# Strassen's seven block products for the up-projections of the second block's feed-forwards

## The chip, the cores and the metric

The kernel runs on one core of a Trainium2 chip. TensorE (PE) multiplies, VectorE (DVE), ScalarE (ACT) and GpSimd (POOL) do the elementwise work, and SyncE (SP) issues most of the loads. The metric is the time of one execution on the device, in microseconds (us); the time before is the median of three runs.

## The reference, cut to what matters

Two blocks of two layers each follow one another on 512 tokens of 1024 features, all in float32. The change touches only the feed-forward of the second block, which runs once in each of its two layers:

```python
# D_MODEL = 1024, D_FF = 2816, CONV_WIDTH = 3
def conv_glu_ffn(x, w_up, conv_w, conv_b, w_down):
    S = x.shape[1]
    h = x @ w_up
    a, b = h[..., :D_FF], h[..., D_FF:]
    ap = jnp.pad(a, ((0, 0), (CONV_WIDTH - 1, 0), (0, 0)))
    conv = conv_b + ap[:, 0:S] * conv_w[0]
    for j in range(1, CONV_WIDTH):
        conv = conv + ap[:, j:j + S] * conv_w[j]
    return (jax.nn.silu(conv) * b) @ w_down

# in each layer, behind the mixer:
x = x + conv_glu_ffn(rms_norm_2(x, norm2_g), w_up, conv_w, conv_b, w_down)
```

## The kernel before, in words

**Products.** Activations lie feature-major: a tile holds 128 features by 512 tokens. Every float32 operand of a large product is split into two float32r parts, hi (a rounded copy, ScalarE) and lo (the exact rest, `x - hi`, VectorE), and a product is three matmuls, hi·hi, hi·lo and lo·hi. A matmul has a stationary 128 by 128 block of weights and a moving tile of up to 512 tokens. All matmuls are issued by the helper `mm`, line L164.

**Weights.** `wget` (L269) loads a tile of 2048 numbers a partition into one of two buffers named raw (SP's queue), and `wsplit` (L256) makes whi (L260, ScalarE) and wlo (L261, VectorE), two buffers each. Up-projection tiles are 8 k-tiles by 256 columns; tiles of the product back (`w_down`) are 4 k-tiles by 256 columns.

**The feed-forward, `ffn2` (L1702).** The mixer's last product goes by `by_segment` (L311) over two segments of 256 tokens, and `rms` (L324) behind each segment sums the squares of the new residual and makes r = 1 / rms. `gained` (L1264) makes the feed-forward's input from `x * gain`, without r; r is multiplied in behind the up-products (L1722 on VectorE for the convolution's half, L1728 on GpSimd for the gate's). For each of 11 pairs of feature tiles, `up` takes one weight tile of the convolution's half and one of the gate's half: 4 output tiles of 8 k-tiles by 3 matmuls of 512 tokens, 96 matmuls. The convolution is one ScalarE instruction and two of VectorE (L1725, L1726), then SiLU; the gate multiplies (L1731), and the result is split into "g" (L358). `chunks` (L1143) takes the pairs in groups of 2, 2, 2, 2, 2 and 1; the product back of a group (`down`, four weight tiles of 24 matmuls of 512 tokens, added to the residual on VectorE, L1747) comes in one piece behind the first pair of the next group. The last group's product back goes by segment again (L1738).

**Order.** The order of the instructions on each engine is fixed when the kernel is built, by a planner that follows dependences, free buffers and the order of the program with its own estimates of durations. Each engine then works its list off in order. Small tiles of 256 columns come from a rotation of three buffers (`small`, L321), which the sums of squares use too; tiles of 512 columns for scratch come from a rotation of five (`tmp`).

## Time and profile before

| | |
|---|---|
| median of 3 runs | 3603.54 us (3602.54 to 3608.32) |
| span of the profiled execution | 3595.4 us |
| what lies around that span, against the median | 8.1 us |
| PE, weight loads, DVE, ACT, POOL busy | 96%, 80%, 65%, 38%, 22% of the span |
| feed-forward of the second block, each layer | 377 us of the span |

The profile is one execution. Busy shares are averages over stages with different limits; a stage's own row tells what limits it. A matmul's recorded duration overlaps the next one's, so the pace of PE is read from the distance of starts.

### The profile page before, as it was taken

The numbers are of one execution on the slowest core, as the hardware profiler recorded it, in microseconds if no ns is written. First come the engines' busy times: TensorE is split into PE (matmuls) and PEld (weight loads), VectorE is DVE, ScalarE is ACT, GpSimd is POOL, SyncE is SP. The second block draws the span as 40 slices with busy tenths as digits, with TensorE's granted clock in tenths as the row PEclk, the third lists the DMA queues.
The fourth block names the chain that finished last, engine by engine and source line by source line (L and its number), as shares of the span: only waits on it lengthen the run. The fifth ranks groups of instructions, "written<-read, shape, count | busy, mean of one in ns | idle before, by whom it ended". The sixth has DMA issues, their size and how long they took to land.

```text
span 3595.4 us, 46792 instructions
## 1 busy us (share of the span) xinstructions
PE 3446.1 (96%) x18150; PEld 2868.4 (80%) x18150; DVE 2319.3 (65%) x3809; ACT 1380.5 (38%) x2141; POOL 803.9 (22%) x812
## 2 busy tenths in 40 slices
PE   7998999999999999999999999979999999999998
PEld 5787888888888887877887887866888876778887
DVE  5458865557786765565757556797654569865454
ACT  4234545242222234355543334425422343453223
POOL 2232322320000022312321001563100126521101
PEclk9999999999999999999999999989999999899999
DMA  6376543423233323763433233443132252512232
GB/s 222 115 235 182 160 129 107 137 70 107 87 125 122 125 81 118 230 163 103 134 130 122 88 117 99 132 146 101 65 106 94 82 166 86 179 60 88 88 106 70
DMA packets 358589, 438.52 MB, mean 122 GB/s; under 512 B 41342, under 2 KB 310288, under 8 KB 358368
## 3 DMA queue, kind: packets, MB, share of 16 engines
q1 hardware_dynamic: 327648, 345.48, 32.0%
q0 software_dynamic: 19200, 71.17, 5.7%
q10 hardware_dynamic: 11520, 18.89, 1.6%
q8 instruction: 143, 2.34, 0.3%
q14 instruction: 78, 0.64, 0.1%
HBM read 363.78 MB, written 71.70 MB: 121 GB/s over the span
## 4 chain that ended last, share of the span: by engine, by line
PE 67%; DVE 8%; issue 2%; ACT 1%; DMA 1%; POOL 0%; DVEq 0%; SPq 0%; ACTq 0%; POOLq 0%
PE d L164 40%; PE s L164 19%; PE n L164 4%; DVE sc L1393 1%; PE o L164 1%; DVE wlo L261 1%; DVE m L1392 1%; PE g L164 1%; PE d L177 1%; PE b L177 1%; DVE hl L368 0%; DVE tmp L1324 0%; ACT whi L260 0%; DVE att L1486 0%; DVE pt L1554 0%
## 5 line engine op out<-in xcount | busy, mean ns | idle before, releaser
L164 PE MATMUL d<-h,whi 128*128 128x512 f32 (+2 forms) x2896 | 894.3, 392 | 16.3 <-DVE h L1271 6.1
L260 ACT CAST whi<-raw 128x2048 fp32r<-128x2048 f32 (+2 forms) x271 | 422.2, 1558 | 696.2 <-PE d L164 400.1
L164 PEld LDWEIGHTS d<-h,whi 128*128 128x128 f32 (+1 forms) x2896 | 539.8, 190 | 146.7 <-DVE h L1271 9.4
L261 DVE TENSOR_TENSOR wlo<-raw,whi 128x2048 fp32r<-128x2048 f32 (+2 forms) x255 | 484.3, 1899 | 234.9 <-ACT whi L260 233.2
L164 PE MATMUL d<-h,wlo 128*128 128x512 f32 (+2 forms) x1448 | 560.6, 391 | 1.4 <-DVE wlo L261 1.4
L164 PE MATMUL s<-h,whi 128*128 128x256 f32 (+3 forms) x2176 | 528.7, 335 | 12.8 <-ACT whi L260 6.5
L164 PEld LDWEIGHTS s<-h,whi 128*128 128x128 f32 (+1 forms) x2176 | 370.0, 189 | 60.4 <-ACT whi L260 6.8
L164 PE MATMUL s<-h,wlo 128*128 128x256 f32 (+3 forms) x1088 | 361.6, 333 | 2.3 <-DVE wlo L261 2.3
L164 PE MATMUL d<-g,whi 128*128 128x512 f32 (+1 forms) x1200 | 338.5, 374 | 6.1 <-DVE x L1070 2.3
L164 PEld LDWEIGHTS d<-h,wlo 128*128 128x128 f32 (+1 forms) x1448 | 275.1, 190 | 63.3 <-DVE wlo L261 1.8
L164 PEld LDWEIGHTS d<-g,whi 128*128 128x128 f32 x1200 | 216.9, 188 | 52.8 <-issue 2.8
L164 PEld LDWEIGHTS s<-h,wlo 128*128 128x128 f32 (+1 forms) x1088 | 205.7, 189 | 24.6 <-DVE wlo L261 3.0
L164 PE MATMUL n<-h,whi 128*128 128x512 f32 (+1 forms) x768 | 218.5, 367 | 4.6 <-ACT tmp L975 3.1
L164 PE MATMUL d<-g,wlo 128*128 128x512 f32 (+1 forms) x600 | 213.9, 373 | 0.0
L1728 POOL TENSOR_TENSOR ya<-ya,r 128x512 f32<-128x512 f32 x44 | 75.2, 1710 | 577.5 <-ACT ya L1727 577.5
L619 ACT ACTIVATE e<-s,sm 128x768 f32<-128x768 f32 (+1 forms) x160 | 130.9, 819 | 116.3 <-DVE sm L617 88.0
L164 PE MATMUL s<-ku,ku 96*128 96x512 f32 (+3 forms) x720 | 154.2, 345 | 17.6 <-ACT e L619 14.4
L164 PE MATMUL s<-g,whi 128*128 128x256 f32 (+1 forms) x688 | 168.2, 335 | 0.0
L617 DVE TENSOR_REDUCE sm<-s 128x1 f32<-128x768 f32 (+1 forms) x160 | 134.1, 844 | 50.3 <-PE s L164 48.7
L164 PEld LDWEIGHTS n<-h,whi 128*128 128x128 f32 x768 | 135.9, 192 | 26.6 <-ACT tmp L975 4.7
L164 PEld LDWEIGHTS s<-ku,ku 96*128 96x128 f32 (+1 forms) x720 | 120.7, 190 | 42.3 <-ACT e L619 18.8
L164 PE MATMUL d<-whi,h 128*128 128x256 f32 x768 | 147.9, 288 | 0.0
(472 smaller groups left out, 6315.6 us busy)
## 6 DMA issues: line engine op xcount, KB each, us to landing
raw<-in__w_up SPq DMA_DIRECT2D x88, 1024.0 KB, 5.1
raw<-in__w_in SPq DMA_DIRECT2D x53, 1024.0 KB, 5.4
raw<-in__w_down SPq DMA_DIRECT2D x80, 512.0 KB, 3.4
araw<-in__w_ada SPq DMA_DIRECT2D x28, 1024.0 KB, 5.4
raw<-in__w_out SPq DMA_DIRECT2D x16, 1024.0 KB, 5.0
raw<-in__w_ada SPq DMA_DIRECT2D x15, 1024.0 KB, 9.5
U<-qd SPq DMA_DIRECT2D x32, 256.0 KB, 4.6
qd<-hl POOLq DMA_DIRECT2D x14, 512.0 KB, 4.5
```

The source lines that it names most:

```text
L164: self.last = self.nc.tensor.matmul(*a, **k)
L177: return self.nc.tensor.transpose(*a, **k)
L260: self.nc.scalar.copy(hi, raw[:, 0:n])
L261: (self.nc.gpsimd if self.wpool else self.nc.vector).tensor_tensor(lo, raw[:, 0:n], hi.bitcast(F32), op=OP.subtract)
L617: nc.vector.tensor_reduce(m[:, 0:1], s, axis=AX.X, op=OP.max, negate=True)
L619: nc.scalar.activation(e, s, AF.Exp, bias=m[:, 0:1], accum_out=m[:, 1:2])
L1392: nc.vector.max(m8[t], sc[t])
L1393: nc.vector.match_replace(sc[t], m8[t], sc[t], TAKEN)
L1728: nc.gpsimd.tensor_tensor(t_, t_, r, op=OP.mult)
```

## The change

The up-projection of a weight tile is written as a product of 2 by 2 blocks: k in two halves of four k-tiles, columns in two halves of 128, tokens in two halves of 256. Instead of the eight block products, seven are made (a11, a12, a22 and the sums s1 to s4 of weight blocks, against blocks of the input and its sums T), each 4 k-tiles by 3 matmuls of 256 tokens, 84 matmuls a weight tile. The sums of weight blocks are four GpSimd instructions a tile, and their splits are two casts and two subtractions more; the results are put together by five VectorE instructions and two ScalarE copies from PSUM.

The first `NPLAIN` = 2 pairs of each layer (four weight tiles) are made without it, by `plain`, with matmuls of 256 tokens, all features of the first token half ahead of the second; meanwhile the generator `sums` makes T. The input is made by `halved` in place of `gained`, and it has r in it, so that the multiplications by r behind the products go. The products back of a group stand one by one behind the weight tiles of the next group. The product with s4 of a tile, `last`, is held back (`owed`) until the product back behind that tile has been issued, and the convolution or the gate of the tile follows it. The last output tile takes the place of the weight sums, and the load of the final gains moves from the start of `ffn2` to its end. Comments and docstrings go as well, so lines shift.

```diff
...
+NPLAIN = 2
...
+    def halved(self, x, r, scale, bias, fp, gtag, gbufs):
+        nc = self.nc
+        H = S // 2
+        B = [[[None] * 4 for _ in range(2)] for _ in range(2)]
+        for k in range(KD):
+            j, kk = k // 4, k % 4
+            hs = [self.t(fp, [P, S if j else H], F32R, "hb" if j else "ha", 8) for _ in range(2)]
+            B[j][0][kk] = [h[:, 0:H] for h in hs]
+            if j:
+                B[1][1][kk] = [h[:, H:S] for h in hs]
+            else:
+                both = self.t(fp, [P, S], F32R, gtag, gbufs)
+                B[0][1][kk] = [both[:, 0:H], both[:, H:S]]
+        T = [[self.t(fp, [P, 4, H], F32R, "ht", 8) for _ in range(2)] for _ in range(4)]
+        for n in range(2):
+            c = slice(n * H, (n + 1) * H)
+            for k in range(KD):
+                hi, lo = B[k // 4][n][k % 4]
+                v = self.small(H)
+                if k % 2:
+                    nc.gpsimd.tensor_tensor(v, x[k][:, c], r[:, c], op=OP.mult)
+                    if bias is None:
+                        nc.scalar.activation(v, v, AF.Copy, scale=scale(k))
+                    else:
+                        nc.scalar.activation(v, v, AF.Identity, scale=scale(k), bias=bias(k))
+                    nc.scalar.copy(hi, v)
+                    nc.vector.tensor_tensor(lo, v, hi.bitcast(F32), op=OP.subtract)
+                else:
+                    nc.vector.scalar_tensor_tensor(v, x[k][:, c], scale(k), r[:, c], op0=OP.mult, op1=OP.mult)
+                    if bias is None:
+                        nc.scalar.copy(hi, v)
+                        nc.vector.tensor_tensor(lo, v, hi.bitcast(F32), op=OP.subtract)
+                    else:
+                        nc.scalar.activation(hi, v, AF.Identity, bias=bias(k))
+                        nc.vector.scalar_tensor_tensor(lo, v, bias(k), hi.bitcast(F32), op0=OP.add, op1=OP.subtract)
+        def sums():
+            for kk in range(4):
+                u = []
+                for k in (kk, kk + 4):
+                    u.append(self.tmp(S))
+                    nc.gpsimd.tensor_tensor(u[-1], x[k], r, op=OP.mult)
+                    if bias is None:
+                        nc.scalar.activation(u[-1], u[-1], AF.Copy, scale=scale(k))
+                    else:
+                        nc.scalar.activation(u[-1], u[-1], AF.Identity, scale=scale(k), bias=bias(k))
+                b11, b12, b21, b22 = u[0][:, 0:H], u[0][:, H:S], u[1][:, 0:H], u[1][:, H:S]
+                a, b = self.tmp(S), self.tmp(S)
+                t1, t3, t4, t2 = a[:, 0:H], a[:, H:S], b[:, 0:H], b[:, H:S]
+                nc.gpsimd.tensor_tensor(t1, b11, b12, op=OP.subtract)
+                nc.gpsimd.tensor_tensor(t3, b22, b12, op=OP.subtract)
+                nc.gpsimd.tensor_tensor(t2, b22, t1, op=OP.add)
+                nc.gpsimd.tensor_tensor(t4, t2, b21, op=OP.subtract)
+                hi, lo = T[kk]
+                nc.scalar.copy(hi[:, 0:2, :], a.rearrange("p (i n) -> p i n", i=2))
+                nc.vector.tensor_tensor(lo[:, 0:2, :], a.rearrange("p (i n) -> p i n", i=2), hi[:, 0:2, :].bitcast(F32), op=OP.subtract)
+                nc.scalar.copy(hi[:, 2, :], t4)
+                nc.vector.tensor_tensor(lo[:, 2, :], t4, hi[:, 2, :].bitcast(F32), op=OP.subtract)
+                nc.scalar.activation(hi[:, 3, :], t2, AF.Copy, scale=-1.0)
+                nc.vector.scalar_tensor_tensor(lo[:, 3, :], t2, -1.0, hi[:, 3, :].bitcast(F32), op0=OP.mult, op1=OP.subtract)
+                yield
+        return B, T, sums()
+    def strassen_setup(self, B, T, fp):
+        self.sB, self.sT = B, T
+        self.sraw = self.t(fp, [P, 4, 512], F32, "sraw", 1)
+        self.shi = self.t(fp, [P, 5, 512], F32R, "shi", 1)
+        self.slo = self.t(fp, [P, 5, 512], F32R, "slo", 1)
+        self.fp, self.owed, self.odd = fp, None, 0
+    def plain(self, ws, n=2):
+        H = S // 2
+        pss = [self.pd() for _ in ws]
+        for t in range(2):
+            for (w, j), ps in zip(ws, pss):
+                for k in range(KD):
+                    bh, bl = self.sB[k // 4][t][k % 4]
+                    wh, wl = [x[:, k, j * P:(j + 1) * P] for x in w]
+                    for i, (a, b) in enumerate(((wh, bh), (wh, bl), (wl, bh))):
+                        self.mm(ps[:, t * H:(t + 1) * H], a, b, start=(k == 0 and i == 0), stop=(k == KD - 1 and i == 2))
+        return pss
+    def strassen_weights(self, ap2d, c0):
+        nc = self.nc
+        raw, self.ahead = self.ahead or self.wload(self.raw(), ap2d, 0, KD, c0, 256), None
+        rv = raw.rearrange("p (k n) -> p k n", k=KD)
+        blk = lambda t, i, j: t[:, 4 * j:4 * j + 4, P * i:P * i + P]
+        hi, lo = [self.t(self.wp, [P, 2048], F32R, tag, 2).rearrange("p (k n) -> p k n", k=KD) for tag in ("whi", "wlo")]
+        for v in (lambda t: t[:, :, 0:P], lambda t: blk(t, 1, 1)):
+            nc.scalar.copy(v(hi), v(rv))
+            nc.vector.tensor_tensor(v(lo), v(rv), v(hi).bitcast(F32), op=OP.subtract)
+        o, self.odd = self.odd, 1 - self.odd
+        sv = lambda t, i: t[:, i, :].rearrange("p (k n) -> p k n", k=4)
+        s2, s4, s3, s1 = [sv(self.sraw, i) for i in (o, 1 - o, 2, 3)]
+        nc.gpsimd.tensor_tensor(s3, blk(rv, 0, 0), blk(rv, 1, 0), op=OP.add)
+        nc.gpsimd.tensor_tensor(s1, blk(rv, 1, 0), blk(rv, 1, 1), op=OP.add)
+        nc.gpsimd.tensor_tensor(s2, s1, blk(rv, 0, 0), op=OP.add)
+        nc.gpsimd.tensor_tensor(s4, s2, blk(rv, 0, 1), op=OP.add)
+        for c, d in ((slice(2, 4), slice(3, 5)), (slice(0, 2), slice(1 - o, 3 - o))):
+            nc.scalar.copy(self.shi[:, d, :], self.sraw[:, c, :])
+            nc.vector.tensor_tensor(self.slo[:, d, :], self.sraw[:, c, :], self.shi[:, d, :].bitcast(F32), op=OP.subtract)
+        s2, s4, s3, s1 = [[sv(t, i) for t in (self.shi, self.slo)] for i in (1, 2 - 2 * o, 3, 4)]
+        return {"a11": [blk(hi, 0, 0), blk(lo, 0, 0)], "a12": [blk(hi, 0, 1), blk(lo, 0, 1)], "a22": [blk(hi, 1, 1), blk(lo, 1, 1)],
+                "s3": s3, "s1": s1, "s2": s2, "s4": s4}
+    def block_product(self, ps, w, x, first=True):
+        for k in range(4):
+            (wh, wl), (xh, xl) = [t[:, k, :] for t in w], x(k)
+            for i, (a, b) in enumerate(((wh, xh), (wh, xl), (wl, xh))):
+                self.mm(ps, a, b, start=(first and k == 0 and i == 0), stop=(k == 3 and i == 2), skip_group_check=not first)
+    def settle(self):
+        if self.owed is not None:
+            go, self.owed = self.owed, None
+            go()
+    def strassen(self, w, use):
+        nc = self.nc
+        H = S // 2
+        B, T = self.sB, self.sT
+        b = lambda j, n: lambda k: B[j][n][k]
+        t = lambda i: lambda k: [p[:, i, :] for p in T[k]]
+        row = lambda: self.t(self.fp, [P, S], F32, "row", 3)
+        bank = lambda: self.pd()[:, 0:H]
+        r0, pa, pb = row(), bank(), bank()
+        self.block_product(pa, w["a11"], b(0, 0))
+        nc.scalar.copy(r0[:, 0:H], pa)
+        self.block_product(pb, w["a12"], b(1, 0))
+        nc.vector.tensor_tensor(r0[:, 0:H], pb, r0[:, 0:H], op=OP.add)
+        self.settle()
+        r1, u2, pc, pdd, pf = row(), self.t(self.fp, [P, H], F32, "uu", 2), bank(), bank(), bank()
+        self.block_product(pc, w["s3"], t(1))
+        self.block_product(pdd, w["s1"], t(0))
+        self.block_product(pa, w["s2"], t(3), first=False)
+        nc.scalar.copy(u2, pa)
+        nc.vector.tensor_tensor(r1[:, 0:H], pc, u2, op=OP.add)
+        nc.vector.scalar_tensor_tensor(r1[:, H:S], r1[:, 0:H], -1.0, pdd, op0=OP.mult, op1=OP.subtract)
+        self.block_product(pf, w["a22"], t(2))
+        nc.vector.scalar_tensor_tensor(r1[:, 0:H], r1[:, 0:H], -1.0, pf, op0=OP.mult, op1=OP.subtract)
+        def last():
+            self.block_product(pdd, w["s4"], b(1, 1), first=False)
+            nc.vector.tensor_tensor(r0[:, H:S], pdd, u2, op=OP.add)
+            use(0, r0)
+            use(1, r1)
+        self.owed = last
     def ffn2(self, l, x):
         nc, a, col = self.nc, self.a, self.cols
         with ExitStack() as es:
             fp = self.pool(es, "fp", self.other())
...
+            gain = col["norm2"]
+            B, T, sums = self.halved(x, self.r2, lambda k: gain[:, k:k + 1], None, fp, "g", 12)
+            self.strassen_setup(B, T, fp)
             (w0, w1, w2), cb = self.cw, col["conv_b"]
...
+            gt, ya = {}, {}
+            def conv(f, u):
+                t_ = ya[f] = self.t(fp, [P, S], F32, "ya", 2)
+                nc.scalar.activation(t_, u, AF.Identity, scale=w2[:, f:f + 1], bias=cb[:, f:f + 1])
+                nc.vector.scalar_tensor_tensor(t_[:, 1:S], u[:, 0:S - 1], w1[:, f:f + 1], t_[:, 1:S], op0=OP.mult, op1=OP.add)
+                nc.vector.scalar_tensor_tensor(t_[:, 2:S], u[:, 0:S - 2], w0[:, f:f + 1], t_[:, 2:S], op0=OP.mult, op1=OP.add)
+                nc.scalar.activation(t_, t_, AF.Silu)
+            def gate(f, u):
+                t_ = ya.pop(f)
+                nc.vector.tensor_tensor(t_, u, t_, op=OP.mult)
+                gt[f] = self.split(fp, t_, S, "g", 12)
+            def up(p0, c0, use):
+                if p0 < NPLAIN:
+                    w = self.wget(a["w_up_2"][l], 0, KD, c0, 256)
+                    for j, ps in enumerate(self.plain([(w, 0), (w, 1)])):
+                        use(2 * p0 + j, ps)
+                    next(sums, None)
+                else:
+                    w = self.strassen_weights(a["w_up_2"][l], c0)
+                    self.strassen(w, lambda j, row: use(2 * p0 + j, row))
+            def down(f0, nk, g):
+                w = self.wget(a["w_down_2"][l], f0 * P, nk, g * 256, 256)
+                for j in range(2):
+                    m = 2 * g + j
+                    ps = self.pd()
+                    self.dense(w, j * P, P, gt, f0, nk, S, ps)
+                    nc.vector.tensor_tensor(x[m], ps, x[m], op=OP.add)
+            todo, f0 = [], 0
+            for npair in (2, 2, 2, 2, 2, 1):
+                per = len(todo) // (2 * npair)
+                for p0 in range(f0 // 2, f0 // 2 + npair):
+                    for c0, use in ((p0 * 256, conv), (F + p0 * 256, gate)):
+                        up(p0, c0, use)
+                        for _ in range(per):
+                            todo.pop(0)()
+                            self.settle()
+                todo = [lambda f=f0, g=g: down(f, 4, g) for g in range(4)]
+                f0 += 2 * npair
+            self.settle()
+            f0, nk = f0 - 2, 2
+            w = self.wget(a["w_down_2"][l], f0 * P, nk, 0, D)
+            self.banks(**(MIX2 if l < DEPTH - 1 else LAST))
             if l == DEPTH - 1:
...
+                gb = self.t(fp, [P, S], F32, "row", 3)
                 nc.gpsimd.dma_start(gb, a["final_norm_g_2"].rearrange("(o n) -> o n", o=1)[:, 512:D].to_broadcast([P, 512]))
...
+            self.by_segment(w, range(KD), gt, f0, nk, S, lambda m, ps, si, c: nc.vector.tensor_tensor(
+                x[m][:, c], ps, x[m][:, c], op=OP.add), self.rms(x, self.r2) if l < DEPTH - 1 else self.last_rows(x, fp, gb))
...
-                o = self.t(pool, [P, D], F32, "out", 2)
+                o = self.sraw.rearrange("p a n -> p (a n)")[:, t * D:(t + 1) * D]
...
```

## Rows read from the trace of the kernel before

**Rows 1.** The page's first part: busy time, share, instructions.

```profile
PE 3446.1 (96%) x18150; PEld 2868.4 (80%) x18150; DVE 2319.3 (65%) x3809; ACT 1380.5 (38%) x2141; POOL 803.9 (22%) x812
```

**Rows 2.** Windows: stretch, length, busy PE PEld DVE ACT POOL, clock, DMA.

```profile
2536.00:2913.00 377.00, 374.26 (x1673) 302.98 (x1671) 201.09 (x240) 125.25 (x145) 47.05 (x37) 1.00 0.30 95
3206.00:3583.00 377.00, 376.09 (x1705) 305.90 (x1704) 196.67 (x237) 124.88 (x150) 43.51 (x29) 1.00 0.26 85
2585.38:2652.58 67.20, 67.20 (x290) 53.98 (x289) 33.45 (x37) 19.79 (x20) 6.75 (x5) 1.00 0.30 94
```

**Rows 3.** Timeline of POOL in the first feed-forward: start, duration, work.

```profile
2585.38 2.87 POOL L1728 TENSOR_TENSOR ya<-ya,r 128x512 f32<-128x512 f32 x1 [12.76 <-ACT ya L1727]
2592.80 1.29 POOL L1728 TENSOR_TENSOR ya<-ya,r 128x512 f32<-128x512 f32 x1 [4.54 <-ACT ya L1727]
...
2652.58 2.87 POOL L1728 TENSOR_TENSOR ya<-ya,r 128x512 f32<-128x512 f32 x1 [13.88 <-ACT ya L1727]
```

**Rows 4.** Timeline of PE where matmuls have 256 columns, two places.

```profile
1838.18 0.28 PE L164 MATMUL d<-mg,wlo 128*128 128x256 f32 x1
...
1842.14 0.28 PE L164 MATMUL d<-mg,wlo 128*128 128x256 f32 x1
...
2898.20 0.28 PE L164 MATMUL d<-g,wlo 128*128 128x256 f32 x1
...
2903.80 0.28 PE L164 MATMUL d<-g,wlo 128*128 128x256 f32 x1
```

**Rows 5.** Groups by line and shape in 2556 to 2912 us: busy, mean ns.

```profile
L1747 DVE TENSOR_TENSOR x<-d,x 128x512 f32<-128x512 f32 x40 | 27.6, 690 | 44.4 <-PE d L164 44.4
L261 DVE TENSOR_TENSOR wlo<-raw,whi 128x1024 fp32r<-128x1024 f32 x20 | 24.5, 1225 | 2.9 <-ACT whi L260 2.4
L1726 DVE SCALAR_TENSOR_TENSOR ya<-u,colsw,ya 128x510 f32<-128x510 f32 x21 | 15.7, 749 | 0.7
...
L1738 DVE TENSOR_TENSOR x<-d,x 128x256 f32<-128x256 f32 x15 | 6.3, 422 | 2.9 <-PE d L164 2.9
L338 POOL TENSOR_TENSOR small<-small,tmp 128x256 f32<-128x256 f32 x6 | 4.7, 782 | 32.4 <-ACT tmp L336 28.0 <-ACT small L336 4.3
```

**Rows 6.** Timeline of DVE at three places.

```profile
2489.88 0.69 DVE L1625 TENSOR_TENSOR x<-d,x 128x512 f32<-128x512 f32 x1 [0.27 <-PE d L164]
...
2584.81 2.29 DVE L261 TENSOR_TENSOR wlo<-raw,whi 128x2048 fp32r<-128x2048 f32 x1 [1.86 <-ACT whi L260]
...
3012.53 6.77 DVE L261 TENSOR_TENSOR wlo<-raw,whi 128x2048 fp32r<-128x2048 f32 x1
```

**Rows 7.** Timeline of POOL at two of these places.

```profile
2489.49 1.30 POOL L1532 TENSOR_TENSOR qm<-qm,gt 128x512 f32<-128x512 f32 x1 [4.43 <-DVE gt L1531]
...
3012.27 2.41 POOL L1479 TENSOR_TENSOR qx<-qm,gt 128x1024 f32<-128x1024 f32 x1
3014.63 1.30 POOL L1477 TENSOR_TENSOR gt<-kb,gt 128x512 f32<-128x512 f32 x1
3015.88 1.26 POOL L1546 TENSOR_TENSOR pt<-pt 128x504 f32<-128x504 f32 x1
```

**Rows 8.** Timeline of PE where a feed-forward begins: first block's, then second's.

```profile
1848.94 0.59 PE L164 MATMUL n<-small,ones 128*128 128x256 f32 x2
1851.38 0.73 PE L164 MATMUL d<-h,whi 128*128 128x256 f32 x4 [1.85 <-ACT h L594]
...
1855.71 0.39 PE L164 MATMUL d<-h,whi 128*128 128x256 f32 x2
...
2536.13 0.58 PE L164 MATMUL d<-h,whi 128*128 128x256 f32 x2
```

**Rows 9.** Timeline of DVE: r of the second token half completed.

```profile
2551.86 0.42 DVE L395 SCALAR_TENSOR_TENSOR r<-small,r 128x256 f32<-128x256 f32 x1
```

**Rows 10.** Windows, the columns of Rows 2: the first block's feed-forward begins.

```profile
1849.00:1856.00 7.00, 5.09 (x22) 4.06 (x22) 6.84 (x11) 6.09 (x12) 2.37 (x4) 0.76 0.69 217
```

38 lines of the change are left out of this document (removed).

## Prediction, made before the changed kernel ran

> **What bounds the kernel now.** The page comes first: PE is busy for 96% of the span [rows 1]. That alone does not say that PE sets the pace, so the windows come next. Both feed-forwards of the second block last 377 us each with PE busy for 374 and 376, at the full granted clock (1.00, the 2.4 GHz level), while DVE works about half the time [rows 2]. The third reading is a pace. The GpSimd instruction behind a SiLU recurs at 2585.38 and 2652.58 [rows 3], 67.20 us apart: one group of two pairs, by the code 4 x 48 up-matmuls and 96 of the product back. 67.20 / 288 = 0.2333 us for a matmul of 512 tokens, without a hole. So here a matmul left out is time saved, until another engine becomes slower than PE.
>
> **What the products save.** The price of a matmul of 256 tokens stands in two places [rows 4]. From 2898.20 to 2903.80 there are 16 triples, 48 matmuls: 5.60 / 48 = 0.1167 us, exactly half of 0.2333. From 1838.18 to 1842.14 there are 33: 3.96 / 33 = 0.1200. The first has the same kind of operands in the same phase, so I take 0.1175. A weight tile is now 48 x 0.2333 = 11.20 us and becomes 84 x 0.1175 = 9.87 (9.80 to 10.08). Each layer has 22 weight tiles, 4 of them plain, so 36 tiles in all gain 1.33 us: **-47.9 us** (-40.3 to -50.4). The 8 plain tiles become 96 x 0.1175 = 11.28: **+0.6** (0 to +2.6).
>
> **Steady state: DVE and GpSimd.** A Strassen tile and the product back behind it will take PE 9.87 + 24 x 0.2333 = 15.47 us (16.80 before). In that time DVE has, by [rows 5], the lo parts of 3584 weights (3 x 1.23 and, at 512, 0.69: 4.4), of the product back's weights 1.23, two additions to the residual 1.38, five half-width instructions from PSUM 5 x 0.42 = 2.1, and the convolution 4 x 0.75 or the gate 4 x 0.69, 2.9 on average: 12.0 us, where 33.45 / 4 = 8.4 stand now [rows 2]. GpSimd has four sums at 1.29 [rows 3]: 5.2 us. ACT, now at 19.79 / 4 = 4.9 [rows 2], gains 1.5 casts of 1024 and two copies and stays near 8.
>
> 12.0 and 5.2 each fit into 15.47, but they don't always run side by side. The subtraction at 2584.81 ends at 2587.10 [rows 6]; the GpSimd instruction that starts in it takes 2.87 instead of 1.29 and ends 1.15 behind it [rows 3]. The other way round, a subtraction at 3012.53 that takes 2.29 elsewhere takes 6.77 [rows 6], while three GpSimd instructions in a row end at 3017.14 [rows 7]; it ends 2.16 after them. An addition from PSUM at 2489.88 takes its 0.69 [rows 6] inside a GpSimd instruction of 1.30 [rows 7]. So a DVE instruction with two inputs in SBUF and a GpSimd instruction exclude each other; one with an input in PSUM is free. The Trainium skill states this (SBUF — State Buffer, section Who interferes with whom): two SBUF inputs on VectorE contend with a GpSimd read, and the loser waits for the whole instruction. The trace agrees in both directions.
>
> Of DVE's 12.0 us 3.5 are free of it. If nothing of GpSimd's work were covered, the pair would need 17.1 us a tile, 1.65 more than PE: 36 x 1.65 = +59. If all fits, 0. I stay near the fit: DVE's free 3.5 us and its 3.5 idle us together exceed 5.2, GpSimd works a tile ahead, and the next tile's lo parts have from the end of a22 (8.5 us into the tile) to its end. A wait of half an instruction on each of four is about 2.5 us, and 14.5 still fit. I take 0.2 us a tile for collisions: **+7** (0 to +59).
>
> A weight tile's raw buffer is now held until GpSimd's last sum. On SP the next up-load waits for it, and the load of the next `w_down` tile stands behind; that tile is needed 9.9 us later, so I cost this at nothing; if GpSimd falls behind, it is part of the same delay. The load of the final gains moves behind GpSimd's last sums; the last product back (96 matmuls, 11.2 us) covers it.
>
> **Where a feed-forward begins.** Before, the up-products did not need r: the first stands at 2536.13 without idle time before it [rows 8], and r is complete only at 2552.28 [rows 9]. Now they wait for it. The nearest row is the first block's feed-forward, whose input has r in it: behind the last sums at 1848.94 PE idles 1.85 us, and only from 1855.71 do products follow at full pace [rows 8]. In those 6.77 us stand 12 products and 6 matmuls of sums, worth 12 x 0.12 + 6 x 0.25 = 2.9: 3.8 lost, and the granted clock of the stretch is 0.76, a mix of the 1.2 and 2.4 GHz levels [rows 10]. The changed kernel squares all eight tiles, and its `v` share three buffers with those sums, so the third `v` waits for the end of the second half's norm. DVE alone needs 16 x 0.42 + 8 x 0.47 + 2.29 + 1.5 = 14.3 us for the input, against 11.3 of the first plain tile: at least 3. If the three buffers pace the first half, it is 4.4 + (4 x 2.2 + 4 x 1.3) / 3 = 9, where 4.4 is my estimate for addition, square, sum and norm behind the last product (seven instructions of 0.4 to 0.8 in a row), 2.2 and 1.3 for the chains of an odd tile (GpSimd 0.78, two of ACT, DVE 0.42) and an even one (three of about 0.43), all after [rows 5]. I take 6 a layer: **+12** (+6 to +20).
>
> **T, late or not.** T must be there at the first Strassen tile's third product, 6 + 4 x 11.28 + 2.8 = 54 us after the beginning. GpSimd has by then 8 x 0.78 + 4 x (2 x 1.29 + 4 x 0.78) + 2 x 1.29 = 31.6; DVE 40 (input 10.5, three whole weight tiles 6.9, the first Strassen weights 3.1, convolution and gate 11.5, splits of T 6.1, norm 2). Taking turns all the time they need 71.7, 18 late; overlapped, none. I take 4 a layer: **+8** (0 to +36). What waits behind it is PE's whole list, since the first product back stands behind that tile.
>
> **The end.** Behind the last s4 DVE has the gate (3.8 us with ACT's casts), the last weights' lo 2.29 and four additions 2.8, covered by one product back of 5.6: at most 3.3 late. 1.5 a layer: **+3** (0 to +7).
>
> **The sum.** -47.9 + 0.6 + 7 + 12 + 8 + 3 = -17.3. On the profiled span 3595.4 it gives 3578; 8.1 us lie between that span and the median of the runs, so 3603.5 - 17.3 = **3586**.
>
> **Rivals.**
> - *DVE and GpSimd set the pace* (slower). Place: the 36 Strassen tiles, and the making of T. For it: [rows 6, 7], three GpSimd instructions in a row that let DVE through only at the end. Against: two of the four sums depend on the one before, DVE has 3.5 us a tile that need no turn, and nothing that it makes is due at once. All in turns it is +59 in place of +7: 3638. It decides from 0.2 + 17.3 / 36 = 0.7 us of stall a tile on. By the skill's page cited above, applied to every pair of instructions, this would be the outcome.
> - *The beginnings cost double* (+24, and T +16): about 3606, no change. For it: three buffers for a chain that has four of its own in the first block. Against: whole PE tiles stand ready to hide the second half.
> - *All is hidden*: -50.4 + 6 = 3559 to 3568. Against it: PE's idle time in [rows 8].
> - *A matmul of 256 tokens isn't half price in this mix*, because each loads its own weights. 84 of them cost as much as before at 11.20 / 84 = 0.133 us; both rows are below. The Trainium skill (TensorE: Matmul & The Clock Gate, section LDWEIGHTS) prices a load of 128 columns by the columns alone, an estimate of 107 ns at any width of the moving tile; not overlapped, that would double a 256-token matmul and cost some 300 us. The trace does not agree: 0.1167 from start to start.
>
> **How the numbers follow.** PE-bound with the boundary costs above, 3568 to 3596: 0.55, my forecast. All hidden: 0.08. DVE and GpSimd in turns, wholly or in part, 3600 to 3640: 0.22, a quarter of it within 0.2%. Beginnings double: 0.12. Matmuls dearer: 0.03. About 0.2%, 7 us, is what a measurement of this kernel can tell from no change. Faster by more: 0.55 + 0.08 = 0.63. Same: 0.12 + 0.05 = 0.17. Slower: 0.17 + 0.03 = 0.20. The range for 8 in 10 leaves out the fastest part of the hidden case and the slower half of the turns: 3563 to 3620; the forecast's own is 3568 to 3596.
>
> **What the profile after would show.** A group of four Strassen tiles and four products back in 61.9 us instead of 67.20, with PE busy throughout; 84 matmuls a tile at 0.117 to 0.120. DVE near 12 us a tile plus some 2.5 of longer instructions beside GpSimd's 5.2. PE idle for some 6 us at both beginnings, ended by `hi` or `lo` of the input, and a few before the first product with T, ended by a split of T. I am wrong if groups take 65 us or more with PE waiting for lo parts or POOL sums, or if the idle time at a beginning passes 12 us.

## The result, and the profile after

The changed kernel takes 3639.6 us (median of 4 runs, 3637.9 to 3641.7), the kernel before beside it 3603.7: ratio 1.0099 [1.0085, 1.0112]. It is slower by 36 us, and outside the range of 3563 to 3620. The profiled span is 3636.2 us, 40.8 longer than before.

The page's first part, against [rows 1]:

```profile
PE 3435.1 (94%) x19782; PEld 2929.3 (81%) x19782; DVE 2501.4 (69%) x4093; ACT 1483.0 (41%) x2377; POOL 1038.3 (29%) x976
```

Windows of the two feed-forwards and of the first one's Strassen stage, columns as in [rows 2]:

```profile
2537.00:2930.00 393.00, 365.96 (x2479) 332.13 (x2478) 292.42 (x378) 175.97 (x266) 161.28 (x113) 0.98 0.28 90
3230.00:3624.00 394.00, 367.79 (x2513) 334.86 (x2512) 287.57 (x382) 178.73 (x275) 162.51 (x112) 0.98 0.26 83
...
2607.00:2911.00 304.00, 292.08 (x1945) 262.21 (x1945) 219.15 (x285) 123.98 (x175) 111.59 (x67) 1.00 0.30 94
```

PE has less to do and takes longer: 26 to 27 us of each stretch are idle where [rows 2] had 1 to 3. For a ledger I call *lost* the length of a stretch minus its matmuls at the pace of [rows 2], 0.2333 us for 512 columns and half of it for 256; so it holds idle time and also what matmuls take beyond that pace. The feed-forward runs from the mixer's last product to its own last one; two numbers are the two layers, in us.

| | before | after | change |
|---|---|---|---|
| length | 374.4, 376.2 | 393.3, 393.9 | +36.6 |
| matmuls at that pace | 370.9, 371.3 | 345.3, 345.9 | -51.0 |
| lost in the first 50 us | 1.1, 0.4 | 21.7, 19.3 | +39.5 |
| lost after that | 2.4, 4.5 | 26.4, 28.7 | +48.2 |

So the products saved what was forecast, and two other things cost more: the beginnings, and the steady state. Of what is lost after the first 50 us, 24.1 and 24.3 lie between the first Strassen product and the last, 2.2 and 4.3 behind the last, and nothing ahead of the first. (The other 4 us of the span lie outside the feed-forwards.)

**Steady state.** Waits from 2600 to 2880: what the DMA queue of SP, PE and PE's weight loads waited for (us in total, times, longest):

```profile
SPq L266 <- DVE wlo L1799: 213.6, 16, 14.4
...
PE d L165 <- ACT whi L1798: 6.0, 13, 0.8
PE d L165 <- DVE wlo L1799: 5.4, 13, 0.4
...
PEld d L165 <- ACT whi L1798: 11.7, 13, 1.2
PEld d L165 <- DVE wlo L1799: 8.3, 14, 0.6
```

The timelines of SP, POOL, ACT and DVE around one tile (start, duration, work):

```profile
2720.40 0.37 SPq L266 DMA_DIRECT2D raw<-in__w_up  x1
2723.02 0.37 SPq L266 DMA_DIRECT2D raw<-in__w_down  x1
2737.66 0.37 SPq L266 DMA_DIRECT2D raw<-in__w_up  x1
...
2725.70 1.84 POOL L1804 TENSOR_TENSOR sraw<-raw 128x512 f32<-128x512 f32 x1 [10.11 <-DMA raw<-in__w_up]
...
2730.70 2.15 POOL L1807 TENSOR_TENSOR sraw<-sraw,raw 128x512 f32<-128x512 f32 x1
...
2732.89 1.05 ACT L1809 CAST shi<-sraw 128x1024 fp32r<-128x1024 f32 x1 [2.03 <-POOL sraw L1807]
2733.85 0.36 ACT L1846 COPY uu<-d 128x256 f32<-128x256 f32 x1
2734.11 1.57 ACT L1798 CAST whi<-raw 128x1024 fp32r<-128x1024 f32 x2
...
2733.97 1.23 DVE L1810 TENSOR_TENSOR slo<-sraw,shi 128x1024 fp32r<-128x1024 f32 x1 [2.27 <-ACT shi L1809]
...
2735.45 1.22 DVE L1799 TENSOR_TENSOR wlo<-raw,whi 128x1024 fp32r<-128x1024 f32 x1
...
2736.92 0.69 DVE L1799 TENSOR_TENSOR wlo<-raw,whi 128x512 fp32r<-128x512 f32 x1
```

Read them as a circle. The tag `raw` has two buffers, and up-tiles and `w_down` tiles take them in turn, so every up-tile has the same one. Its load is issued at 2720.40, lands and lets GpSimd begin at 2725.70 (5.3 us); the four sums end at 2732.85 (7.15, by turns with VectorE, for 4 x 1.29 = 5.2 alone); only then come the cast and the subtractions that also read `raw`, because in the lists of ScalarE and VectorE they stand behind the casts of the sums; the last ends at 2737.61 (4.8), and at 2737.66 the next load goes out. That is 17.26 us, and PE's work for a tile and its product back is 15.4. From 2651.31 to 2822.81 there are eleven such loads, 17.15 us apart on average: PE does not set the pace, and waits a little for each `whi` and `wlo`. Of the 24.1 us lost in this stage 11.9 are idle PE (304.00 - 292.08); the granted clock is 1.00, and the rest stands inside the recorded times of matmuls, whose weight loads waited for the same two tiles.

**The beginning.** Timelines of PE, ACT, DVE and POOL; the mixer's last product is at 2537.05, against [rows 8, 9]:

```profile
2544.40 2.08 PE L165 MATMUL n<-small,ones 128*128 128x256 f32 x4 [6.88 <-DVE small L339]
2548.32 1.01 PE L165 MATMUL d<-ha,whi 128*128 128x256 f32 x3 [1.85 <-ACT ha L1736]
...
2537.26 1.88 ACT L261 CAST whi<-raw 128x2048 fp32r<-128x2048 f32 x1
2539.16 1.28 ACT L393 ACT_TABLE_LOAD   x1
2540.45 0.47 ACT L393 ACTIVATE r<-n,eps 128x256 f32<-128x256 f32 x1
...
2539.17 2.29 DVE L262 TENSOR_TENSOR wlo<-raw,whi 128x2048 fp32r<-128x2048 f32 x1 [1.19 <-ACT whi L261]
...
2544.27 0.94 DVE L396 SCALAR_TENSOR_TENSOR r<-small,r 128x256 f32<-128x256 f32 x1
...
2541.61 3.32 POOL L339 TENSOR_TENSOR small<-small,tmp 128x256 f32<-128x256 f32 x4 [7.37 <-ACT small L337]
```

Before, products followed without a hole. Now PE idles 6.88 us for the second half's squares and 1.85 for the first `ha`. Ahead of the norm stand the split of the second plain weight tile (1.88 and 2.29 us) and a table load of 1.28, and VectorE's instruction of 0.42 us [rows 9] takes 0.94 beside GpSimd's additions. PE is idle for 13.9 us of the first 50 (its window stands under "The beginnings": 36.13 busy); the other 7.8 of the 21.7 lost are matmuls slower than the pace of [rows 2], at a granted clock of 0.83. No product with T waits.

### The profile page after: what moved, and what is told of

Same layout as the page of the kernel before. It is cut to its first block, busy times and chain, and to the rows that moved or that the text cites. A ratio compares the mean times of both kernels' runs of the same rounds, so it can differ in the third digit from the quotient of the medians.

```text
span 3636.2 us, 51011 instructions
## 1 busy us (share of the span) xinstructions
PE 3435.1 (94%) x19782; PEld 2929.3 (81%) x19782; DVE 2501.4 (69%) x4093; ACT 1483.0 (41%) x2377; POOL 1038.3 (29%) x976
## 4 chain that ended last, share of the span: by engine, by line
PE 51%; DVE 13%; DMA 5%; issue 4%; POOL 4%; ACT 2%; SPq 0%; DVEq 0%; ACTq 0%; POOLq 0%
PE d L165 25%; PE s L165 18%; PE n L165 4%; DMA raw<-in__w_up 3%; POOL sraw L1807 2%; DVE wlo L262 1%; DVE wlo L1799 1%; POOL sraw L1805 1%; PE o L165 1%; DVE sc L1394 1%; POOL sraw L1806 1%; PE g L165 1%; DVE m L1393 1%; ACT shi L1809 1%; PE d L178 1%
## 5 line engine op out<-in xcount | busy, mean ns | idle before, releaser
L261 ACT CAST whi<-raw 128x2048 fp32r<-128x2048 f32 (+2 forms) x235 | 353.4, 1504 | 487.6 <-PE s L165 247.3
L262 DVE TENSOR_TENSOR wlo<-raw,whi 128x2048 fp32r<-128x2048 f32 (+2 forms) x219 | 405.4, 1851 | 182.8 <-ACT whi L261 182.0
L165 PE MATMUL d<-h,whi 128*128 128x512 f32 (+2 forms) x1456 | 451.8, 392 | 16.4 <-DVE h L1272 6.1
L165 PEld LDWEIGHTS s<-h,whi 128*128 128x128 f32 (+1 forms) x2176 | 370.9, 190 | 59.0 <-ACT whi L261 6.8
L165 PE MATMUL d<-g,whi 128*128 128x512 f32 (+1 forms) x1328 | 369.2, 365 | 6.1 <-DVE x L1071 2.3
L165 PEld LDWEIGHTS d<-h,whi 128*128 128x128 f32 (+1 forms) x1456 | 272.1, 192 | 84.7 <-DVE h L1272 8.9
L165 PE MATMUL d<-h,wlo 128*128 128x512 f32 (+2 forms) x728 | 283.1, 392 | 1.3 <-DVE wlo L262 1.3
L1810 DVE TENSOR_TENSOR slo<-sraw,shi 128x1024 fp32r<-128x1024 f32 x72 | 94.7, 1315 | 137.8 <-ACT shi L1809 137.8
L339 POOL TENSOR_TENSOR small<-small,tmp 128x256 f32<-128x256 f32 x36 | 28.3, 786 | 521.2 <-ACT tmp L337 496.1
L165 PEld LDWEIGHTS d<-h,wlo 128*128 128x128 f32 (+1 forms) x728 | 139.8, 192 | 31.6 <-DVE wlo L262 1.8
L165 PE MATMUL d<-ht,shi 128*128 128x256 f32 x864 | 158.7, 283 | 0.0
L1804 POOL TENSOR_TENSOR sraw<-raw 128x512 f32<-128x512 f32 x36 | 54.9, 1526 | 360.0 <-DMA raw<-in__w_up 292.1
```

The source lines that it names most:

```text
L165: self.last = self.nc.tensor.matmul(*a, **k)
L261: self.nc.scalar.copy(hi, raw[:, 0:n])
L262: (self.nc.gpsimd if self.wpool else self.nc.vector).tensor_tensor(lo, raw[:, 0:n], hi.bitcast(F32), op=OP.subtract)
L1804: nc.gpsimd.tensor_tensor(s3, blk(rv, 0, 0), blk(rv, 1, 0), op=OP.add)
L1810: nc.vector.tensor_tensor(self.slo[:, d, :], self.sraw[:, c, :], self.shi[:, d, :].bitcast(F32), op=OP.subtract)
```

## Experiments

All are edits of the changed kernel, and their ratios go to runs of the kernel before beside them. Lost is counted as above: in the first 50 us of the two feed-forwards, and in the whole of both.

| kernel | us | lost, first 50 | lost, all |
|---|---|---|---|
| before | 3603.7 | 1.1, 0.4 | 8.4 |
| after | 3639.6 | 21.7, 19.3 | 96.1 |
| e1_raw2 | 3598.3 | 23.2, 21.0 | 56.0 |
| e2_order | 3596.6 | 23.2, 19.4 | 54.9 |
| e3_dve | 3596.3 | 23.3, 21.0 | 56.4 |
| e4_vbuf | 3635.1 | 15.5, 13.7 | 91.7 |
| e5_both | 3590.7 | 15.5, 12.9 | 48.6 |
| e6_rready | 3594.1 | 16.4, 18.5 | 47.3 |
| e7_split | 3590.9 | 15.2, 15.8 | 44.1 |
| e8_noT | 3592.6 | 19.2, 17.9 | 49.5 |
| e9_keep | 3594.2 | 20.1, 18.9 | 51.1 |
| e10_lateR | 3606.2 | 19.1, 21.1 | 62.3 |
| e12_noT_late | 3583.0 | 14.1, 13.1 | 39.3 |
| e13_split_rready | 3582.4 | 14.5, 14.8 | 41.6 |
| e14_lateR_noT | 3580.3 | 10.9, 14.9 | 38.4 |
| e15_rready_noT | 3570.3 | 8.2, 8.0 | 28.3 |
| e16_lateR_tlate | 3608.1 | 14.7, 17.1 | 67.3 |
| e17_split_tlate | 3587.8 | 15.4, 16.5 | 46.1 |

The time is a median over runs, what is lost comes from the one profiled execution. For all of the changed kernels here the time is 3540 to 3547 us plus what is lost: the ledger accounts for it to a few us, and differences below that are not read.

### The circle around the raw buffer

**e1_raw2**: the `w_down` tiles come in two halves through scratch tiles, so that up-tiles have both raw buffers; every other instruction stays.

```diff
-w = self.wget(a["w_down_2"][l], f0 * P, nk, g * 256, 256)
+hi, lo = ...
+for i in range(2):
+    raw, c = self.wload(self.tmp(S), ...), slice(512 * i, 512 * i + 512)
+    nc.scalar.copy(hi[:, c], raw)
+    nc.vector.tensor_tensor(lo[:, c], raw, hi[:, c].bitcast(F32), op=OP.subtract)
```

> Weights of the products back are loaded in two halves into scratch tiles, so that up-projection tiles have both raw buffers; all sums, splits and products stay. Theory A (one raw buffer is loaded, summed by GpSimd, cast, and only then reloaded, a closed loop of about 17.1 us a tile): a Strassen tile with its product back falls from about 17.1 us to 15.4 to 15.7, and the whole to about 3595 to 3605. Theory B (VectorE and GpSimd exclude each other, 12.0 + 5.2 = 17.2 us of work a tile): all that work stays, so the tile stays near 17.1 and the whole near 3640.

**e2_order**: nothing but the order; the two casts to `shi` and the two subtractions to `slo` of a tile are issued behind those to its own `whi` and `wlo`.

```diff
+with self.tc.issue_after(ia.ins), self.tc.issue_after(iv.ins):
     nc.scalar.copy(self.shi[:, d, :], ...)
     nc.vector.tensor_tensor(self.slo[:, d, :], ...)
```

> The casts and subtractions of a tile's weight sums are issued behind those of the tile's own weights on ScalarE and VectorE; nothing else changes. Theory A: the raw buffer is free once GpSimd's sums are done instead of 4.8 us later, the loop is 5.3 + 7.2 = 12.5 us, and the tile falls to 15.4 to 15.7, the whole to about 3595 to 3605. Theory B: the same work takes the same turns, tile near 17.1, whole near 3640.

**e3_dve**: the four sums on VectorE (`nc.gpsimd` to `nc.vector` in four lines).

> The four weight sums of a tile are made by VectorE instead of GpSimd. Theory A: the loop loses GpSimd's 7.2 us and gains about 3 on VectorE, 5.3 + 3 + 4.8 = 13, so PE paces again unless VectorE, now at 14.8 us of work a tile, falls behind: tile 15.5 to 16.2, whole 3600 to 3620. Theory B: no turns are left, 14.8 us of VectorE fit into 15.4, the same 15.5. If neither holds and the order of the lists is what costs, it stays at 3640.

All three broke the circle: ratios to before 0.999 [0.9981, 0.9999], 0.9982 [0.9973, 0.9992] and 0.9985 [0.9975, 0.9995]; lost in the Strassen stage 2.6 to 2.8 us a layer where 24.2 stood. Windows of that stage, of e1_raw2, e2_order and e3_dve:

```profile
2609.00:2891.00 282.00, 282.00 (x1940) 261.10 (x1940) 234.71 (x302) 127.84 (x194) 117.19 (x64) 1.00 0.29 94
```

```profile
2613.00:2895.50 282.50, 282.50 (x1944) 261.58 (x1944) 230.57 (x285) 124.75 (x175) 98.56 (x65) 1.00 0.32 101
```

```profile
2615.00:2897.00 282.00, 282.00 (x1941) 261.13 (x1940) 233.75 (x348) 124.14 (x175) 0.00 (x0) 1.00 0.32 101
```

PE has no hole, though in the first two GpSimd and VectorE do all their work, with their turns. So the turns do not set the pace by themselves; in the changed kernel they lengthened the sums inside the circle. In e2_order eleven up-loads from 2652.75 to 2808.28 are 15.55 us apart. e3_dve fits both theories; e1_raw2 and e2_order decide between them, since both leave the turns in place.

### The beginnings

**e4_vbuf** gives `v` of `halved` buffers of its own (those of `row` and `uu`, idle then) in place of the three that the norm uses:

```diff
-v = self.small(H)
+v = self.t(fp, [P, S], F32, "row", 3)[:, 0:H] if k % 2 else self.t(fp, [P, H], F32, "uu", 2)
```

> The scratch tiles of the feed-forward's input come from five buffers of their own instead of the three that the sums of squares use. Theory S1 (those three hold the input back): the first product with the input comes about 2 us earlier, the next two stretches lose some 5 us less, and the whole falls by 10 to 15 us to about 3627. Theory S2 (the norm itself is late, behind a weight split, a table load and turns with GpSimd): less than 4 us in all, about 3637.

**e5_both** is e2_order and e4_vbuf together.

> The sums' casts behind the tile's own (as in e2_order) and v in buffers of its own (as in e4_vbuf), together. If the closed loop of the raw buffer only hid what v's buffers give back at the two beginnings, both gains add: e2_order stood at 3596.6 with 23 and 19 us lost in the first 50 us of the two feed-forwards, and the trace of e4_vbuf shows 15.5 and 13.7 there, so about 13 us less than e2_order: 3583 to 3588. Rival: the input's chain only moves, and T or the first Strassen tile's sums are late in its place: 3592 to 3597, with the 13 us found again as idle PE between the plain tiles and the fourth Strassen tile.

Each beginning lost 6 us less in e4_vbuf, but the time fell by 4.5 only (ratio 1.009 [1.0073, 1.0108]): the Strassen stages lost 26.8 and 29.1 in place of 24.1 and 24.3. That fits a circle that PE does not lead. Without the circle it counts, but in the first layer alone: e5_both is at 0.9968 [0.9956, 0.998] and loses 20 and 28 us in the two layers, e2_order 28 and 26. That is less than expected; in the second layer the first Strassen tile waits 5.2 us for a copy of ScalarE that stands behind the cast of a gate.

**e6_rready** and **e7_split** ask what the remaining 13 to 16 us are. e6_rready: `self.halved(x, self.rm, ...)` in place of `self.r2`, where `rm` is the 1/rms of the first block's end, complete long before (so the output is another one). e7_split takes the second plain tile's split out of the norm's way:

```diff
+if between is not None and (n, k) == (1, 4):
+    with self.placed("AV"):
+        between()    # wget of the second plain tile
```

> As e5_both, but the feed-forward's input is multiplied by the 1/rms of the first block's end, a tile that has long been complete, in place of this norm's r (so the output is another one; the norm itself is still computed, and every instruction stays). If the wait for r is what a beginning costs, the first product with ha follows the mixer's last within 3 us, the loss of the first 50 us falls from some 15 to 2 to 5 a layer, and the time is about 20 to 25 us below e5_both. Rival: the making of the input (eight tiles of VectorE, ScalarE and GpSimd work, some 14 us of VectorE by the prediction) sets the beginning by itself: PE still waits for ha, hb and g, 8 to 12 us a layer stay lost, and the time is 5 to 12 us below e5_both.

> As e5_both, but the split of the second plain weight tile (ScalarE 1.88 us, VectorE 2.29 us) is issued behind the fourth input tile of the second half, in place of ahead of the norm of the first half. If it stands in r's way, the first product with ha comes 2 to 4 us earlier in each layer and the time is 4 to 7 us below e5_both. Rival: r waits for the additions in turn with GpSimd anyway, or the second plain tile's products now wait for their lo part: within 2 us of e5_both, or above it.

Both gave nothing against e5_both: 0.997 [0.996, 0.9979] and 0.9968 [0.9955, 0.998]. In the first layer of e7_split the first `ha` product came 3.2 us earlier after the mixer's last than in e5_both, and waits for `g` took it back; in the second it came 1.1 later. So the wait for r was not it, or not alone, and the suspicion fell on turns with GpSimd: in e6_rready it was busy for 9.25 us of the 10 from 2551, and VectorE for 9.96.

**e8_noT** (on e7_split) makes T without GpSimd (another output); **e9_keep** (on e7_split, all computed) keeps `v` and lets T's sums read it:

```diff
-u.append(self.tmp(S))                                      # e8
-nc.gpsimd.tensor_tensor(u[-1], x[k], r, op=OP.mult)
-nc.scalar.activation(u[-1], u[-1], AF.Copy, scale=scale(k))
+nc.scalar.activation(u[-1], x[k], AF.Copy, scale=scale(k))
...
-v = ...                                                    # e9
+v = U[k][:, c]
...
+u = [U[kk], U[kk + 4]]
```

> As e7_split, but T is made without GpSimd: its products with r and its four sums are left out, and T's tiles are scaled copies of x (so the output is another one). PE, VectorE and SP keep every instruction, ScalarE keeps all but changes its inputs. If VectorE's turns with GpSimd pace a beginning (VectorE and GpSimd were both busy for over 90% from 2551 to 2561 of e6_rready, and 256-column instructions of 0.42 us took 0.95), the loss of the first 50 us falls from 15.5 to 6 to 9 us a layer, and the time is 13 to 18 us below e7_split: 3573 to 3578. Rival: the chain of norm, input and split is long by itself: the loss stays at 12 or more and the time within 6 us of e7_split.

> As e7_split, but the scaled input of a feed-forward is made once: each v is kept whole (in the space that the sums' parts of the first Strassen tile take later), and T's sums read it, in place of multiplying x by r again. Out go 8 GpSimd instructions of 1.29 to 1.7 us and 8 of ScalarE of 0.7 a layer; the result is the same. If turns pace the beginning, a third of GpSimd's work there is gone: 2 to 5 us a layer, 3581 to 3587. Rival: the first Strassen tile's casts now wait for T, or the removed multiplications lay in GpSimd's free time: within 2 us of e7_split, or above it.

By the numbers both came out on the side of their rivals, but more is lost than in e7_split, which the rivals do not explain. DVE's timeline of e8_noT shows what else had changed:

```profile
2542.63 1.90 DVE L1737 SCALAR_TENSOR_TENSOR uu<-x,cols,r 128x256 f32<-128x256 f32 x2
2544.46 1.22 DVE L1756 TENSOR_TENSOR ht<-tmp,ht 128x512 fp32r<-128x512 f32 x1
2545.60 0.94 DVE L1740 TENSOR_TENSOR ha<-uu,ha 128x256 fp32r<-128x256 f32 x1
```

T no longer waited for r, so its splits moved up in the list, ahead of the input that PE waits for. In e9_keep the last instruction for r of the second half starts 17.8 us after the mixer's last product, in e7_split 15.3. Neither run tells the theories apart; an edit to what an instruction reads had changed the order of the lists.

**e10_lateR** (on e5_both, all computed) starts as the kernel before did: the first two plain tiles read x times the gain, and r comes behind their products. **e12_noT_late** is e8_noT with T's work behind the input on ScalarE and VectorE.

```diff
+h = self.gained(x, gain, fp, [hs[2 * k:2 * k + 2] for k in range(KD)])    # e10
+self.dense(w, j * P, P, h, 0, KD, S, ps, ...)
+nc.vector.tensor_tensor(u, ps, self.r2, op=OP.mult)
...
+for i_ in last:                                                           # e12
+    es.enter_context(self.tc.issue_after(i_))
```

> On e5_both: the first two plain tiles of each feed-forward read x times its gain without r, split as in the kernel before, and r is multiplied in behind the product (256 columns at a time from the first half of x on); the halves with r, and T, are made during these 22 us. The 16 unscaled tiles lie in the space that the sums and their parts take later. If a beginning costs 16 us because its first products wait for a norm and an input that take two serial turns over VectorE and ScalarE, nearly all of it comes back: 2 to 5 us lost in the first 50, and 3563 to 3570 in all. Rival: VectorE has 10 us more to do before the first product with T (16 subtractions of 0.47 us and four products with r of 0.69), and the loss reappears as a wait for ha, hb or T between 22 and 60 us into the feed-forward: 3578 to 3592.

> As e8_noT (T without GpSimd, another output), with all of T's casts and subtractions behind the whole input on ScalarE and VectorE, where e8_noT had ht ahead of ha. If turns with GpSimd lengthen the making of the input, the loss of the first 50 us falls below e7_split's 15.5 a layer, to 9 to 12, and the time to 3574 to 3582. Rival: T's work on GpSimd plays no part in the beginning, only the order of the lists did in e8_noT: the loss goes back to 14.5 to 16.5, and the time to 3585 to 3590.

**e11_lateR3** is e10_lateR with `NPLAIN = 3`.

> As e10_lateR with a third plain pair, so that T is due 22 us later and 4 tiles of the kernel go back from 84 products of 256 columns to 96: +1.4 us each by rows of before. If T is not late in e10_lateR, this one is 4 to 7 us above it. Rival: T is late there by more than that, and this one is below it.

e10_lateR (3606.2 us, 1.0012 [1.0002, 1.0021]) went its rival's way, and beyond the rival's 3592: 8.0 and 9.6 lost in the first 30 us, then 14 and 13 between 30 and 60, with waits for `whi`, `wlo`, `ha` and `hb`. e11_lateR3 (3604.2 us, 1.0007 [0.9997, 1.0016]) pays 5.6 us more for products and loses 7 less, so it tells little. e12_noT_late (0.9945 [0.9931, 0.996]) loses 1.1 and 2.7 us less than e7_split, between its two sides and nearer to the rival. **e13_split_rready** is e7_split with the ready r of e6_rready, **e14_lateR_noT** e10_lateR with T as in e12_noT_late.

> e7_split with the ready 1/rms of e6_rready in place of this norm's r (so another output; every instruction stays). If the wait for r makes the 13 to 16 us that a beginning still loses, and e6_rready only kept them because the second weight tile's split stood ahead of the input, the loss of the first 50 us falls to 3 to 7 us a layer and the time to 3566 to 3577. Rival: the input's own instructions, in the same lists as the norm's additions and squares, make it: 11 us or more stay lost, and the time is 3582 or more.

> e10_lateR with T made without GpSimd, behind the input (another output), as in e12_noT_late. In e10_lateR VectorE and GpSimd are both busy for 94 to 97% from 2560 to 2602 and PE loses 14 us there. If turns set the pace of that stretch, the loss between 30 and 60 us falls from 14 to 4 or less, and the time by 18 to 25 us, to 3580 to 3588. Rival: VectorE's own work is too much for the stretch: 9 us or more stay lost a layer, and the time is 3594 or more.

With r ready and the split away, 14.5 and 14.8 stay lost, the rival's side; the time fell 8 us, of which the ledger places 2.5 in the feed-forwards. e14_lateR_noT did as the turns say: from 30 to 60 us 4.0 and 5.2 lost instead of 14 and 13. Part of that is T's later place in the lists, which e16_lateR_tlate below has with GpSimd at work: it loses 8.1 and 11.7 there. Windows of the same 42 us in e10_lateR and in e14_lateR_noT:

```profile
2560.00:2602.00 42.00, 32.66 (x196) 29.39 (x195) 39.45 (x38) 23.78 (x44) 40.76 (x32) 0.88 0.12 38
```

```profile
2555.50:2597.50 42.00, 38.99 (x285) 36.36 (x284) 38.54 (x51) 33.48 (x63) 19.26 (x15) 1.00 0.20 63
```

VectorE is as busy in both, but gets through 38 instructions beside GpSimd and 51 without. That left one possibility for the beginning: two causes, each hidden behind the other. **e15_rready_noT** takes both away (e13_split_rready and e12_noT_late together).

> e13_split_rready and e12_noT_late together: r is a ready tile and T is made without GpSimd, behind the input (another output). If the norm's chain and VectorE's turns with GpSimd cover each other, the loss of the first 50 us falls from 14.5 and 13.6 to 5 to 9 us a layer, 10 to 18 us in all: 3566 to 3573. Rival: the input's own work on VectorE and ScalarE, with the norm's squares and additions between, holds PE by itself: 11 us or more stay lost, 3578 or more.

It held: 8.2 and 8.0 lost, 0.9905 [0.9891, 0.9918]. Windows of the first 50 us of after, e7_split, e12_noT_late, e13_split_rready and e15_rready_noT:

```profile
2537.00:2587.00 50.00, 36.13 (x244) 33.88 (x243) 46.12 (x51) 32.53 (x59) 38.81 (x36) 0.83 0.13 42
```

```profile
2538.80:2588.80 50.00, 41.03 (x300) 38.32 (x299) 44.24 (x52) 32.17 (x58) 39.03 (x34) 0.90 0.14 43
```

```profile
2542.20:2592.20 50.00, 41.66 (x310) 39.67 (x309) 38.43 (x59) 34.93 (x65) 16.17 (x16) 0.90 0.17 53
```

```profile
2537.20:2587.20 50.00, 41.51 (x306) 38.63 (x305) 47.30 (x53) 32.25 (x61) 44.25 (x38) 0.93 0.16 53
```

```profile
2539.00:2589.00 50.00, 45.24 (x360) 43.75 (x359) 43.86 (x64) 37.83 (x69) 16.69 (x16) 0.97 0.22 73
```

The count behind PE's busy time is what it got done: 300 in e7_split, 310 with one cause gone, 306 with the other, 360 without both. The granted clock, 1.00 in [rows 2], is 0.83 in after's stretch, a mix of its levels 1.2 and 2.4 GHz behind the waits, and 0.97 in the last: part of the loss is matmuls at the lower level. In the first layer PE's idle time in these five is 13.9, 9.0, 8.3, 8.5 and 4.8 us; the rest of what is lost (7.8, 6.2, 5.8, 6.0 and 3.4) goes with the lower clock, so an idle us saved here gives back more than itself.

That it is the turns which hold e13_split_rready shows on VectorE. From the mixer's last addition to the split of the second plain tile it has no hole, and works 20 us on what takes it 14.6 in e15_rready_noT (with one subtraction more in e13_split_rready); windows of e13_split_rready and e15_rready_noT:

```profile
2538.10:2558.15 20.05, 13.40 (x72) 11.15 (x72) 19.84 (x27) 13.37 (x31) 16.95 (x19) 0.83 0.00 0
```

```profile
2539.90:2554.50 14.60, 10.24 (x63) 9.24 (x64) 14.60 (x26) 11.08 (x26) 10.13 (x12) 0.88 0.00 1
```

Not tested is a ready r with T made in full by GpSimd behind the input, which would part the turns from T's place in GpSimd's list. What PE still waits for in e15_rready_noT are the first input tiles:

```profile
PE d L165 <- ACT ha L1739: 3.0, 1, 3.0
PE d L165 <- DVE ha L1740: 1.1, 1, 1.1
PE d L165 <- DVE g L1740: 0.6, 1, 0.6
```

Last, the order of T alone in kernels that compute everything: **e16_lateR_tlate** is e10_lateR, **e17_split_tlate** e7_split, each with T's work behind the input on GpSimd, ScalarE and VectorE.

> e10_lateR, all of it computed, with T's work behind the whole input on GpSimd, ScalarE and VectorE. If the loss between 30 and 60 us (11 to 13 a layer) comes from GpSimd's T work amid the input of the second plain pair, that stretch gives back 4 to 8 us a layer, and T is late by less than that: 3590 to 3600. Rival: T is then late at the first Strassen tile by as much: 3600 to 3608.

> e7_split, all of it computed, with T's work behind the whole input in the same way. e12_noT_late, without T's GpSimd work, lost 14.1 and 13.1 us a beginning where e7_split lost 15.2 and 15.8: so at most 4 us in all come back, 3586 to 3591. Rival: T is late at the first Strassen tile instead: 3591 to 3600.

e16_lateR_tlate fell to its rival (1.0007 [0.9998, 1.0016]): 4.6 us a layer come back between 30 and 50 us, and 6 to 8 more are lost between 50 and 100, where T is late. e17_split_tlate has the lowest time of those that compute everything: 0.9953 [0.994, 0.9967], 17 us below the kernel before and 52 below the change. The time lies in the forecast range, but that it beats e5_both and e7_split is not shown: their intervals overlap with its own, and its trace loses 2 us more than that of e7_split.

## Why the prediction was wrong, point by point

- **The products: right.** -47.9 and +0.6 were forecast, -51.0 is in the ledger. The 256-column matmul costs 0.1167 us here too, and 96 of them no more than 48 of 512 columns: PE has no hole in the Strassen stages of e1_raw2 to e3_dve, and 2.6 to 2.8 us a layer are lost there.
- **The raw buffer: the step that failed.** "if GpSimd falls behind, it is part of the same delay", it says, and the wait was costed at nothing. GpSimd did not fall behind; its sums are one link of a circle: load 5.3, sums 7.15, casts and subtractions 4.8, on a buffer that the code's alternation makes a single one. With +7 forecast for the whole steady state, the ledger has +48, all of it in the Strassen stages. By these numbers the circle without turns would be 5.3 + 5.2 + 4.8 = 15.3 us, PE's 15.4 with nothing to spare, so the 2 us that the turns add to the sums would go straight to the end; this is an estimate, no run has the circle without turns. e2_order, which only moves a tile's two casts and two subtractions, shows that the order makes it a circle of that length. One sign of being wrong that the prediction names came so: four tiles take 4 x 17.15 = 68.6 us, over its 65.
- **Collisions in the steady state: right in kind, but not where they cost.** Outside the circle they cost nothing that shows: the Strassen stage loses 2.7 us a layer in e3_dve, without a turn, and 2.8 in e2_order, with all of them (3.6 were forecast). The Trainium skill (SBUF — State Buffer, Who interferes with whom) has a VectorE instruction with two inputs in SBUF contend with a GpSimd instruction that reads SBUF; the durations agree (1.84 and 2.15 us for GpSimd's 1.29), but the end does not follow from it: PE had no hole in e2_order.
- **The beginnings: the second step that failed, a term mis-sized.** 6 us a layer were forecast for the beginning and 4 for a late T; 20.6 and 18.9 were measured, all of it at the beginning, and T was not late. PE's idle time there, 13.9 and 13.5, is over the 12 that the prediction names as its other sign of being wrong. The three buffers of `v`, priced as a pace of 9 us in the prediction, cost 6 a layer by e4_vbuf and e5_both. The wait for r and the turns with GpSimd over T cost 7 to 8 a layer together, and taking one away gives 0.7 to 2.7. The rival "The beginnings cost double" had the size, +40, but put 16 of it on T, and had nothing for the steady state.
- **The end: no change** (2.2 and 4.3 lost behind the last Strassen product, about what the kernel before loses after its beginning), +3 forecast.
- **The rival "DVE and GpSimd set the pace"** gave 3638, the right time for the wrong reason: it priced 59 us of turns in the steady state and kept the beginnings at +20. The turns were not the limit there; they are one of two in the beginning, and a part of what e10_lateR loses.

That e13_split_rready is 8 us faster than e7_split, when its feed-forwards lose 2.5 less, is not credited to the edit. The two profiled executions are 6.8 us apart: 2.5 in the feed-forwards, 1.6 ahead of the first one, and 2.8 between the two, in a stretch that lasts 297.1 to 301.5 us from trace to trace though no edit is made in it. What makes that stretch longer or shorter stays open.

## What to carry to other kernels

For every buffer that is loaded again, add up one round: load, all its readers in the order in which the engines' lists hold them, next load. If the round is near the pace of the bottleneck engine, look at which reader stands behind work that it does not need. And where two causes of a wait overlap, taking away one can show next to nothing: try both before calling either innocent.

## What the runs showed of the hardware

VectorE has a two-input addition of 128x512 cheaper than GpSimd (0.69 us against 1.29), and giving it GpSimd's four sums a tile cost VectorE next to nothing. Groups of e3_dve by line and shape in its Strassen stage (busy, mean ns):

```profile
L1873 DVE SCALAR_TENSOR_TENSOR ya<-row,colsw,ya 128x511 f32<-128x511 f32 x18 | 13.3, 745 | 0.0
...
L1804 DVE TENSOR_TENSOR sraw<-raw 128x512 f32<-128x512 f32 x16 | 11.0, 690 | 5.6 <-DMA raw<-in__w_up 5.0
```

The same convolution line in e2_order, where GpSimd makes the sums:

```profile
L1874 DVE SCALAR_TENSOR_TENSOR ya<-row,colsw,ya 128x511 f32<-128x511 f32 x18 | 23.9, 1333 | 12.0 <-ACT ya L1873 12.0
```

64 sums of 0.69 us are 44 us of work more, and yet VectorE is busy for 233.75 us in e3_dve and 230.57 in e2_order. Its other instructions are shorter without GpSimd beside them, and that pays for most of the sums: 10.6 us on this line (1333 ns against 745), 10.7 on the second line of the convolution and 10.5 on the subtraction that splits the gated result.
